# Where tiles lie in SBUF modulo 512 bytes, and where the last projection's tiles live

## The chip, the cores and the metric

The kernel runs on one core of one Trainium2 chip. The metric is the device time of one execution in microseconds, the median of repeated runs. One further execution was taken by the hardware profiler, and all rows below are from it.

## The reference

A decoder trunk of two layers on 256 tokens of width 2048. Each layer is `h <- LayerNorm(alpha * h + W_out(gate * mixer(h)))`. Layer 0 is a gated linear recurrence (HGRN2), layer 1 native sparse attention: compressed, selected and windowed keys, whose three outputs are summed under gates. With 256 tokens there are four blocks of 64, so the selection takes them all.

```
def _hgrn2_mixer(x, w_in, g_norm, w_out, lower_bound):
    q, f_logit, v, z = jnp.split(x @ w_in, 4, axis=-1)          # w_in 2048 x 8192
    log_f = jnp.logaddexp(jnp.log(lower_bound), jnp.log1p(-lower_bound) + jax.nn.log_sigmoid(f_logit))
    k = -jnp.expm1(log_f)
    ...                                                          # the recurrence, head by head
    o = o * lax.rsqrt(jnp.mean(o * o, -1, keepdims=True) + RMS_EPS)
    return (o.reshape(B, S, D) * g_norm * jax.nn.silu(z)) @ w_out    # w_out 2048 x 2048

def _nsa_mixer(x, cos, sin, w_in, cmp_pos_k, cmp_w1_k, cmp_w2_k, cmp_pos_v, cmp_w1_v, cmp_w2_v, w_out):
    q, k_c, v_c, k_s, v_s, k_w, v_w, gate_logit, z = jnp.split(x @ w_in, ...)   # w_in 2048 x 7216
    ...
    o = gate(0) * o_cmp + gate(1) * o_slc + gate(2) * o_win
    return (o * jax.nn.silu(z)) @ w_out                          # w_out 2048 x 2048

for i in range(DEPTH):                                           # DEPTH = 2
    h = _layer_norm(DEEPNORM_ALPHA * h + mixer_i(h), ln_g, ln_b)
```

## The kernel before

**Products.** Every product with a weight matrix is done in three passes. An fp32 operand is split into a part `hi` (rounded to fp32r by ScalarE, line 79) and a part `lo = x - hi` (VectorE, line 80), and the product is hi·hi + hi·lo + lo·hi. The weights come in blocks of 256 rows by 512 columns: `load` (line 103) issues one DMA of 512 KB on SP's queue into a `wr` tile, `parts` (line 137) splits it into `wh` and `wl`. One such block is called a j-block here, and a projection has eight of them.

There are two kinds of projection. `project` (line 150, matmuls in lines 146 to 148, and `project_by_tile` likewise) puts tokens on the output's partitions: the activations are the stationary operand, loaded by a weight load of 128x128, and the weights stream past as the moving operand, 512 columns a matmul and twelve matmuls a j-block. `project_t` (line 189, matmuls in lines 201, 203 and 204) puts features on the partitions: the weights are stationary and the activations stream, 256 columns a matmul and 24 matmuls a j-block. The weight load of a matmul runs while the matmul before it streams. So at any time TensorE reads two tiles, one of weights and one of activations.

**Pools and places.** Pools without `side` stack up from the low end of SBUF in the order in which they are opened; those with `side="right"` stack down from the high end. A tag's slots are as large as the largest tile that ever asks for the tag. The *place* of a tile is its byte address in a partition modulo 512. The allocator gives the kernel before these places:

- `acts` (activations, hi and lo of both layers): all slots at 64, 4096 bytes each.
- `wts`: the three `wr` slots at 160. The five `wh` slots at 160, 192, 224, 256, 288 and the five `wl` slots at 320, 352, 384, 416, 448. They step by 32 because `summed` (line 856) asks for 2 x 516 columns under these tags, 4128 bytes, which is eight times 512 plus 32.
- `wide`, in layer 0 and the first product of layer 1: a fourth `wr` and three more `wh` and `wl` slots, in layer 0 all at 160. `slot` (line 127) goes round over the five and the three, so in layer 0 each of a projection's eight j-blocks has its own pair of slots. The order in which they are visited is, as wh/wl: 160/320, 288/448, 256/416, 192/352, 224/384, then three times 160/160.
- `kv`, layer 1: `keys` at 288 and 32, `vals` at 288. In attention `keys` stream against `qT` (at 64), and `pt` (at 256) streams against `vals`.

The *distance* of a matmul is the place of the tile that it streams minus the place of the tile whose weight load runs meanwhile, modulo 512. For instance a matmul of line 147 that streams a `wl` at 320, while activations at 64 are loaded, has distance 256; one of line 201 that streams activations at 64 while a `wh` at 160 is loaded has distance 416. Weights and activations 256 bytes apart give the distance 256 in either kind of projection.

A `wh` tile of the projections with n = 280 columns (lines 705 to 729) has its second row 1120 bytes after the first.

**The order of the work.** The tile framework orders instructions by a timeline simulation of its own, by program order as priority; splits run 300 places ahead (`AHEAD`). SP's queue is served in order, and an issue that waits for its tile holds up all that stand behind it.

**The last projection.** The output projection of layer 1 (lines 873 to 939) works on four column groups c of 512. For c = 0 to 2 it is `project`, c = 3 is `project_by_tile` with `summed`, which needs the splits of all eight j-blocks to be held for a second pass over them. `fetch(c)` (line 838) loads the residual's columns `xr` and two broadcast rows `gb` on SP's queue and applies the rows on GpSimd (lines 846, 847); `gb` has one buffer, `xr` two, in the pool `n1` that takes the place of the attention's pools. After c = 1 `widen()` opens the pool `wide` again (a fourth `wr`, three more `wh` and `wl`), and `row` loads the layer norm's gain and bias, 1 MB each when broadcast. At that stage the activations `hT` in `acts` (tags `ah`, `al`) have been read for the last time.

## Time and profile before

| | |
|---|---|
| median of 3 runs | 1005.46 us (1005.45 to 1005.57) |
| profiled execution | 1005.65 us, of it span 1003.9 us |
| TensorE: matmul (PE) | busy 988.1 us, 98% |
| TensorE: weight load (PEld) | busy 877.3 us, 87% |
| VectorE (DVE) | busy 675.4 us, 67% |
| ScalarE (ACT) | busy 545.3 us, 54% |
| GpSimd (POOL) | busy 118.1 us, 12% |
| granted TensorE clock, mean | 0.997 |
| DMA | 185.25 MB, mean 185 GB/s |

A matmul's end is modelled in the profile and lies after the start of the next one, so the busy time of one matmul (some 390 ns for 512 columns) is longer than the pitch from start to start (some 230 ns). Differences of pitch appear as differences of the mean duration.

### The profile page before, as it was taken

Reading aid. Unit: us, or ns where it says so; the run is one execution under the profiler, and the core shown is the slowest. Engines: PE = TensorE matmul, PEld = TensorE weight load, DVE = VectorE, ACT = ScalarE, POOL = GpSimd, SP = SyncE. Lnnn points to the kernel's source line nnn. Section 1 sums busy time; section 2 is a strip of 40 time slices with the busy share of each in tenths; the row PEclk is TensorE's granted clock in tenths of the full one; section 3 lists DMA queues with packets and bytes.
Section 4 is the critical chain, followed back from the end, with each engine's and each line's share of the span. In section 5 each row is a group of like instructions: output and inputs, shape, how many; then the busy total and the mean of one; then the engine's idle time right before and its main releaser. Section 6 shows DMA issues by size and latency. Waiting matters only on the chain.

```text
span 1003.9 us, 15938 instructions
## 1 busy us (share of the span) xinstructions
PE 988.1 (98%) x6041; PEld 877.3 (87%) x6041; DVE 675.4 (67%) x1123; ACT 545.3 (54%) x872; POOL 118.1 (12%) x180
## 2 busy tenths in 40 slices
PE   8999999999999999999999999999999999999995
PEld 8988998899889988888889888999989889998775
DVE  6796668666765677656575665565858568775578
ACT  6654455444544554434386655554857667775240
POOL 0400300030003000310011020102020022000440
PEclk9999999999999999999999999999999999999998
DMA  8775456556555555457466776666454455345872
GB/s 299 257 232 165 151 180 177 162 155 187 170 166 159 178 179 155 163 172 265 137 217 231 236 241 218 176 209 171 127 167 140 149 154 149 116 142 186 316 247 84
DMA packets 100780, 185.25 MB, mean 185 GB/s; under 512 B 6096, under 2 KB 20512, under 8 KB 100192
## 3 DMA queue, kind: packets, MB, share of 16 engines
q1 hardware_dynamic: 99232, 178.67, 56.7%
q0 software_dynamic: 1472, 5.56, 1.7%
q8 instruction: 47, 0.77, 0.3%
q14 instruction: 29, 0.24, 0.1%
HBM read 180.02 MB, written 4.19 MB: 183 GB/s over the span
## 4 chain that ended last, share of the span: by engine, by line
PE 90%; DMA 4%; DVE 3%; POOL 1%; issue 1%; ACT 1%; SPq 0%; DVEq 0%; POOLq 0%
PE pjb L146 16%; PE pjb L148 16%; PE pjb L147 16%; PE pjb L201 10%; PE pjb L204 10%; PE pjb L203 10%; PE mxb L441 2%; DMA wr<-in_l_w_out_dram 2%; DMA gb<-in_l_ln_g_dram 1%; PE mxb L214 1%; PE mxb L564 1%; PE mxb L565 1%; PE mxb L566 1%; PE mxb L795 1%; DVE wl L80 1%; PE mxb L614 1%
## 5 line engine op out<-in xcount | busy, mean ns | idle before, releaser
L80 DVE TENSOR_TENSOR wl<-wr,wh 128x1024 fp32r<-128x1024 f32 (+2 forms) x305 | 369.5, 1217 | 186.8 <-ACT wh L79 185.2
L79 ACT ACTIVATE wh<-wr 128x1024 fp32r<-128x1024 f32 (+2 forms) x305 | 316.8, 1043 | 307.4 <-PE pjb L148 163.8
L201 PE MATMUL pjb<-ah,wh 128*128 128x256 f32 x832 | 235.1, 284 | 1.4 <-ACT wh L79 1.4
L204 PE MATMUL pjb<-ah,wl 128*128 128x256 f32 x832 | 233.9, 283 | 0.5 <-DVE wl L80 0.5
L203 PE MATMUL pjb<-al,wh 128*128 128x256 f32 x832 | 234.0, 282 | 0.0
L146 PE MATMUL pjb<-wh,ah 128*128 128x512 f32 (+1 forms) x576 | 221.4, 385 | 0.0
L148 PE MATMUL pjb<-wh,al 128*128 128x512 f32 (+1 forms) x576 | 221.2, 384 | 0.0
L147 PE MATMUL pjb<-wl,ah 128*128 128x512 f32 (+1 forms) x576 | 221.0, 384 | 0.0
L201 PEld LDWEIGHTS pjb<-ah,wh 128*128 128x128 f32 x832 | 156.8, 189 | 2.4 <-ACT wh L79 1.9
L203 PEld LDWEIGHTS pjb<-al,wh 128*128 128x128 f32 x832 | 157.0, 189 | 0.5
L204 PEld LDWEIGHTS pjb<-ah,wl 128*128 128x128 f32 x832 | 156.3, 189 | 1.2 <-DVE wl L80 1.1
L148 PEld LDWEIGHTS pjb<-wh,al 128*128 128x128 f32 x576 | 108.2, 188 | 22.0
L146 PEld LDWEIGHTS pjb<-wh,ah 128*128 128x128 f32 x576 | 108.2, 188 | 21.1
L147 PEld LDWEIGHTS pjb<-wl,ah 128*128 128x128 f32 x576 | 108.3, 188 | 20.9
L147 PE MATMUL pjb<-wl,bh 128*128 128x512 f32 (+2 forms) x272 | 104.5, 385 | 2.2 <-DVE wl L80 1.9
L148 PE MATMUL pjb<-wh,bl 128*128 128x512 f32 (+2 forms) x272 | 103.6, 382 | 0.0
L146 PE MATMUL pjb<-wh,bh 128*128 128x512 f32 (+2 forms) x272 | 102.6, 383 | 0.3 <-ACT wh L79 0.3
L147 PEld LDWEIGHTS pjb<-wl,bh 128*128 128x128 f32 x272 | 51.1, 188 | 14.9 <-DVE wl L80 4.8
L146 PEld LDWEIGHTS pjb<-wh,bh 128*128 128x128 f32 x272 | 51.1, 188 | 11.2 <-ACT wh L79 0.8
L148 PEld LDWEIGHTS pjb<-wh,bl 128*128 128x128 f32 x272 | 51.2, 188 | 10.3
L504 POOL TENSOR_TENSOR gz<-gz,gn 128x512 f32<-128x512 f32 x8 | 13.6, 1702 | 314.6 <-ACT gz L503 314.1
L80 DVE TENSOR_TENSOR wl<-ws,wh 128x1024 fp32r<-128x1024 f32 (+2 forms) x33 | 28.2, 863 | 18.4 <-ACT wh L79 18.2
(229 smaller groups left out, 1055.8 us busy)
## 6 DMA issues: line engine op xcount, KB each, us to landing
wr<-in_l_w_in_dram SPq DMA_DIRECT2D x218, 512.0 KB, 3.8
wr<-in_l_w_out_dram SPq DMA_DIRECT2D x64, 512.0 KB, 4.5
ws<-in_l_w_in_dram SPq DMA_DIRECT2D x12, 512.0 KB, 4.5
wr<-in_l_cmp_w_k_dram SPq DMA_DIRECT2D x5, 512.0 KB, 4.0
wr<-in_l_cmp_w_v_dram SPq DMA_DIRECT2D x5, 512.0 KB, 3.9
wr<-in_l_w_in_dram SPq DMA_DIRECT2D x9, 280.0 KB, 3.3
xr<-in_x_dram POOLq DMA_DIRECT2D x4, 512.0 KB, 5.3
norm<-hb POOLq DMA_DIRECT2D x2, 1024.0 KB, 5.5
```

Source lines behind the costliest of these rows:

```text
L79: act.activation(hi, src, AF.Copy)
L80: dve.tensor_tensor(lo, src, hi.bitcast(F32), op=OP.subtract)
L146: pe.matmul(ps, xh, wh, start=(k == 0), stop=False)
L147: pe.matmul(ps, xh, wl, start=False, stop=False)
L148: pe.matmul(ps, xl, wh, start=False, stop=(k == KT - 1))
L201: pe.matmul(o, hi[:, kk, c], xh, start=(k == 0 and b % 2 == 0), stop=False, skip_group_check=True)
L203: pe.matmul(o, hi[:, kk, c], xl, start=False, stop=False, skip_group_check=True)
L204: pe.matmul(o, lo[:, kk, c], xh, start=False, stop=(k == KT - 1), skip_group_check=True)
L214: last[0] = pe.transpose(ps[:, i], src[:, i], ident).ins
L441: pe.matmul(ps[:, h], km[:, h].rearrange("p b r j -> p (b r j)"), later, start=True, stop=True)
L504: pool.tensor_tensor(z, z, gn, op=OP.mult)
L564: pe.matmul(o, a[0], b[0], start=start, stop=False)
```

## The change

- A pool `edge` of 160 bytes is opened at the right edge ahead of `wts`, and `parts` asks for `wh` and `wl` tiles of always 1024 columns, of which it uses the first n of each row. With `summed` gone from these tags their slots have 4096 bytes, eight times 512. So `wr`, `wh` and `wl`, those of `wide` too, all come to place 320: 256 bytes from the activations at 64. In the projections with 280 columns the second row moves to the same place as the first.
- Two gaps in `kv` (320 and 448 bytes) put `keys` at 192 and 448 and `vals` at 0, which is 256 from `pt`.
- The last group: `summed` takes its tiles from a new pool `late` with eight slots each for `wh` and `wl`, opened in the place where `widen()` stood. Its rows have 576 columns, its second half begins at column 320. `wide` is not opened again: from c = 2 on there are three `wr` slots instead of four, and for c = 2 five `wh` and `wl` instead of eight.
- The output projection's loads: `xr` and `gb` of `fetch` become tiles of `acts` under the tag `al` (four slots, so two fetches fit), the layer norm's gain and bias become two halves each under the tag `ah`, loaded by four DMAs of 512 KB instead of two of 1 MB.

No arithmetic is changed. `room` allocates a tile that nothing writes or reads.

```
--- before.py
+++ after.py
@@ -62,6 +62,13 @@
 
     consts = ctx.enter_context(tc.tile_pool(name="consts", bufs=1))
     acts = ctx.enter_context(tc.tile_pool(name="acts", bufs=4))
+
+
+    def room(p, n):
+
+        p.tile([128, n // 4], F32, name=f"room{n}")
+
+    room(ctx.enter_context(tc.tile_pool(name="edge", bufs=1, side="right")), 160)
     wts = ctx.enter_context(tc.tile_pool(name="wts", bufs=5, side="right"))
     pj = ctx.enter_context(tc.tile_pool(name="pj", bufs=4, space=PSUM))
     mx = ctx.enter_context(tc.tile_pool(name="mx", bufs=4, space=PSUM))
@@ -135,8 +142,8 @@
         return p.tile(shape, dtype, name=name, tag=name, bufs=b)
 
     def parts(raw):
-        hi = slot(list(raw.shape), F32R, "wh", 5, 3)
-        lo = slot(list(raw.shape), F32R, "wl", 5, 3)
+        k, n = raw.shape[1:]
+        hi, lo = (slot([128, k, 1024 // k], F32R, name, 5, 3)[:, :, 0:n] for name in ("wh", "wl"))
         with tc.high_priority(AHEAD):
             split(hi, lo, raw)
         return hi, lo
@@ -663,6 +670,7 @@
         kv_pool = attention.enter_context(tc.tile_pool(name="kv", bufs=1, side="right"))
 
         keys = [kv_pool.tile([128, 4, 528], F32R, name=f"keys{i}") for i in range(2)]
+        room(kv_pool, 320)
         vals = [kv_pool.tile([128, NT, 2, 512], F32R, name=f"vals{i}") for i in range(2)]
 
 
@@ -671,6 +679,7 @@
         for v in pcs:
             act.activation(v, ident[:, 0:1, None, None].to_broadcast([128, 2, 2, 64]), AF.Copy, scale=0.0)
         gates = kv_pool.tile([128, NT, 48], F32, name="gates")
+        room(kv_pool, 448)
         ck = Compression(cp, "k")
         ck.flatten(xk)
         xv = cp.tile([128, 4, S], F32, name="xv", tag="xk")
@@ -835,11 +844,11 @@
     stats = n1.tile([128, NT, 8, 6], F32, name="stats", bufs=1)
 
 
+
     def fetch(c):
         cs = slice(512 * c, 512 * (c + 1))
-        xr = n1.tile([128, NT, 512], F32, name="xr")
+        xr, gb = (acts.tile([128, 2, 512], F32, name=name, tag="al") for name in ("xr", "gb"))
         nc.sync.dma_start(xr, norm0[:, cs].rearrange("(t p) d -> p t d", p=128))
-        gb = n1.tile([128, 2, 512], F32, name="gb", bufs=1)
         for i, name in enumerate(("l0_ln_g", "l0_ln_b")):
             nc.sync.dma_start(gb[:, i], a[name][None, cs].to_broadcast([128, 512]))
         for t in range(NT):
@@ -848,27 +857,27 @@
         return xr
 
     def row(name):
-        r = n1.tile([128, D], F32, name=name, bufs=1)
-        nc.sync.dma_start(r, a[name][None, :].to_broadcast([128, D]))
-        return r
-
+        r = [acts.tile([128, D // 2], F32, name=name, tag="ah") for _ in range(2)]
+        for i, v in enumerate(r):
+            nc.sync.dma_start(v, a[name][None, D // 2 * i:D // 2 * (i + 1)].to_broadcast([128, D // 2]))
+        return lambda b, e: r[b * 2 // D][:, b % (D // 2):b % (D // 2) + e - b]
 
     def summed(raw):
 
 
-        parts = [slot([128, 2, 516], F32R, name, 5, 3) for name in ("wh", "wl")]
+        parts = [late.tile([128, 2, 576], F32R, name=name) for name in ("wh", "wl")]
         ws = n1.tile([128, 2], F32, name="ws")
         with tc.high_priority(AHEAD):
-            split(*(bass.AP(tensor=v.tensor, offset=v.offset, ap=[v.ap[0], [516, 2], [258, 2], [1, 256]])
+            split(*(bass.AP(tensor=v.tensor, offset=v.offset, ap=[v.ap[0], [576, 2], [320, 2], [1, 256]])
                     for v in parts), raw.rearrange("p k (u n) -> p k u n", u=2))
             dve.tensor_reduce(ws, raw[:, :, 256:512], axis=AX.X, op=OP.add)
             split(*(v[:, :, 256:258] for v in parts), ws[:, :, None].to_broadcast([128, 2, 2]))
 
         def halves(v, kk):
-            return bass.AP(tensor=v.tensor, offset=v.offset + 516 * kk, ap=[v.ap[0], [258, 2], [1, 256]])
+            return bass.AP(tensor=v.tensor, offset=v.offset + 576 * kk, ap=[v.ap[0], [320, 2], [1, 256]])
 
         return [[halves(v, kk) for v in parts] + [v[:, kk, 0:258] for v in parts] +
-                [v[:, kk, 258:514] for v in parts] for kk in range(2)]
+                [v[:, kk, 320:576] for v in parts] for kk in range(2)]
 
     for c in range(4):
         cs = slice(512 * c, 512 * (c + 1))
@@ -891,12 +900,12 @@
         def centred(t, m, *parts):
             for a, b in parts:
                 h = hb[:, t, a:b]
-                dve.scalar_tensor_tensor(h, h, m, g1[:, a:b], op0=OP.subtract, op1=OP.mult)
+                dve.scalar_tensor_tensor(h, h, m, g1(a, b), op0=OP.subtract, op1=OP.mult)
 
         def scaled(t, r, *parts):
             for a, b in parts:
                 h = hb[:, t, a:b]
-                dve.scalar_tensor_tensor(h, h, r, b1[:, a:b], op0=OP.mult, op1=OP.add)
+                dve.scalar_tensor_tensor(h, h, r, b1(a, b), op0=OP.mult, op1=OP.add)
                 nc.sync.dma_start(y[128 * t:128 * (t + 1), a:b], h)
 
         def finish(t, ps, other=None):
@@ -931,12 +940,11 @@
             if c == 2:
                 last_xr = fetch(3)
             if c == 1:
-                widen()
+                late = ctx.enter_context(tc.tile_pool(name="late", bufs=8, side="right"))
                 g1, b1 = row("l1_ln_g"), row("l1_ln_b")
         else:
             xr.append(last_xr)
             project_by_tile(oT, a["l1_w_out"], 512 * c, finish, summed=summed)
-    wide.close()
 
 
 # ---- launch: one core; inputs and outputs as the reference has them ----
```

## Rows read from the trace of the kernel before

**Rows 1.** The page: busy time of the engines, and the chain that ended last.

```profile
PE 988.1 (98%) x6041; PEld 877.3 (87%) x6041; DVE 675.4 (67%) x1123; ACT 545.3 (54%) x872; POOL 118.1 (12%) x180
...
PE 90%; DMA 4%; DVE 3%; POOL 1%; issue 1%; ACT 1%; SPq 0%; DVEq 0%; POOLq 0%
```

**Rows 2.** Matmuls by line and shape: count, busy us, mean ns, idle before.

```profile
L201 PE MATMUL pjb<-ah,wh 128*128 128x256 f32 x832 | 235.1, 284 | 1.4 <-ACT wh L79 1.4
...
L146 PE MATMUL pjb<-wh,ah 128*128 128x512 f32 x512 | 202.6, 396 | 0.0
...
L147 PE MATMUL pjb<-wl,bh 128*128 128x512 f32 x240 | 95.6, 398 | 2.2 <-DVE wl L80 1.9
```

**Rows 3.** Timeline of PE, layer 0: first matmul of each j-block of one `project_t`.

```profile
132.50 0.28 PE L201 MATMUL pjb<-ah,wh 128*128 128x256 f32 x1
...
135.33 0.28 PE L201 MATMUL pjb<-ah,wh 128*128 128x256 f32 x1
...
138.16 0.28 PE L201 MATMUL pjb<-ah,wh 128*128 128x256 f32 x1
...
140.99 0.28 PE L201 MATMUL pjb<-ah,wh 128*128 128x256 f32 x1
...
143.82 0.29 PE L201 MATMUL pjb<-ah,wh 128*128 128x256 f32 x1
...
146.71 0.28 PE L201 MATMUL pjb<-ah,wh 128*128 128x256 f32 x1
...
149.59 0.28 PE L201 MATMUL pjb<-ah,wh 128*128 128x256 f32 x1
...
152.47 0.28 PE L201 MATMUL pjb<-ah,wh 128*128 128x256 f32 x1
...
155.35 0.40 PE L146 MATMUL pjb<-wh,ah 128*128 128x512 f32 x1
```

**Rows 4.** Groups in 53.86 to 56.63 us, the j-block with slots 160/320.

```profile
L146 PE MATMUL pjb<-wh,ah 128*128 128x512 f32 x4 | 1.6, 397 | 0.0
L148 PE MATMUL pjb<-wh,al 128*128 128x512 f32 x4 | 1.6, 397 | 0.0
L147 PE MATMUL pjb<-wl,ah 128*128 128x512 f32 x4 | 1.6, 390 | 0.0
```

**Rows 5.** The same in 72.89 to 75.67 us, a j-block with slots 160/160.

```profile
L148 PE MATMUL pjb<-wh,al 128*128 128x512 f32 x5 | 2.0, 394 | 0.0
L146 PE MATMUL pjb<-wh,ah 128*128 128x512 f32 x4 | 1.6, 399 | 0.0
L147 PE MATMUL pjb<-wl,ah 128*128 128x512 f32 x4 | 1.6, 392 | 0.0
```

**Rows 6.** Groups in 917 to 985 us, the last projection.

```profile
L147 PE MATMUL pjb<-wl,bh 128*128 128x512 f32 x87 | 34.9, 401 | 2.2 <-DVE wl L80 1.9
...
L146 PE MATMUL pjb<-wh,bh 128*128 128x258 f32 x9 | 2.5, 282 | 0.0
```

**Rows 7.** Stages of the end: us; PE, PEld, DVE, ACT, POOL busy; clock, DMA share, GB/s.

```profile
893.00:917.00 24.00, 24.00 (x119) 19.76 (x118) 13.38 (x22) 14.45 (x27) 0.00 (x0) 1.00 0.52 170
917.00:940.00 23.00, 22.17 (x95) 17.33 (x93) 10.49 (x18) 8.84 (x10) 5.04 (x4) 1.00 0.84 292
```

**Rows 8.** Waits of SP's queue from 880 us: total us, times, longest.

```profile
SPq L844 <- POOL xr L847: 11.4, 3, 5.4
...
SPq L841 <- DVE bl L80: 4.1, 1, 4.1
```

**Rows 9.** Timeline of SP's queue in the same stretch.

```profile
924.06 0.47 SPq L852 DMA_DIRECT2D l_ln_g<-in_l_ln_g_dram  x1
924.57 1.39 SPq L852 DMA_DIRECT2D l_ln_b<-in_l_ln_b_dram  x1
...
959.43 0.34 SPq L844 DMA_DIRECT2D gb<-in_l_ln_g_dram  x1
```

**Rows 10.** What ScalarE's splits waited for, from 915 us.

```profile
ACT wh L79 <- DMA wr<-in_l_w_out_dram: 33.4, 16, 12.0
```

More of the change, by code (lines that the diff above doesn't have):

```diff
@@ L64, in trunk, with room @@
     acts = ctx.enter_context(tc.tile_pool(name="acts", bufs=4))
+    def room(p, n):
+        p.tile([128, n // 4], F32, name=f"room{n}")
+    room(ctx.enter_context(tc.tile_pool(name="edge", bufs=1, side="right")), 160)
     wts = ctx.enter_context(tc.tile_pool(name="wts", bufs=5, side="right"))
@@ L137, in parts @@
     def parts(raw):
-        hi = slot(list(raw.shape), F32R, "wh", 5, 3)
-        lo = slot(list(raw.shape), F32R, "wl", 5, 3)
+        k, n = raw.shape[1:]
+        hi, lo = (slot([128, k, 1024 // k], F32R, name, 5, 3)[:, :, 0:n] for name in ("wh", "wl"))
         with tc.high_priority(AHEAD):
@@ L665, in trunk @@
         keys = [kv_pool.tile([128, 4, 528], F32R, name=f"keys{i}") for i in range(2)]
+        room(kv_pool, 320)
         vals = [kv_pool.tile([128, NT, 2, 512], F32R, name=f"vals{i}") for i in range(2)]
@@ L673, in trunk @@
         gates = kv_pool.tile([128, NT, 48], F32, name="gates")
+        room(kv_pool, 448)
         ck = Compression(cp, "k")
@@ L839, in fetch @@
         cs = slice(512 * c, 512 * (c + 1))
-        xr = n1.tile([128, NT, 512], F32, name="xr")
+        xr, gb = (acts.tile([128, 2, 512], F32, name=name, tag="al") for name in ("xr", "gb"))
         nc.sync.dma_start(xr, norm0[:, cs].rearrange("(t p) d -> p t d", p=128))
-        gb = n1.tile([128, 2, 512], F32, name="gb", bufs=1)
         for i, name in enumerate(("l0_ln_g", "l0_ln_b")):
@@ L850, in row @@
     def row(name):
-        r = n1.tile([128, D], F32, name=name, bufs=1)
-        nc.sync.dma_start(r, a[name][None, :].to_broadcast([128, D]))
-        return r
+        r = [acts.tile([128, D // 2], F32, name=name, tag="ah") for _ in range(2)]
+        for i, v in enumerate(r):
+            nc.sync.dma_start(v, a[name][None, D // 2 * i:D // 2 * (i + 1)].to_broadcast([128, D // 2]))
+        return lambda b, e: r[b * 2 // D][:, b % (D // 2):b % (D // 2) + e - b]
     def summed(raw):
-        parts = [slot([128, 2, 516], F32R, name, 5, 3) for name in ("wh", "wl")]
+        parts = [late.tile([128, 2, 576], F32R, name=name) for name in ("wh", "wl")]
         ws = n1.tile([128, 2], F32, name="ws")
         with tc.high_priority(AHEAD):
-            split(*(bass.AP(tensor=v.tensor, offset=v.offset, ap=[v.ap[0], [516, 2], [258, 2], [1, 256]])
+            split(*(bass.AP(tensor=v.tensor, offset=v.offset, ap=[v.ap[0], [576, 2], [320, 2], [1, 256]])
                     for v in parts), raw.rearrange("p k (u n) -> p k u n", u=2))
@@ L867, in halves @@
         def halves(v, kk):
-            return bass.AP(tensor=v.tensor, offset=v.offset + 516 * kk, ap=[v.ap[0], [258, 2], [1, 256]])
+            return bass.AP(tensor=v.tensor, offset=v.offset + 576 * kk, ap=[v.ap[0], [320, 2], [1, 256]])
         return [[halves(v, kk) for v in parts] + [v[:, kk, 0:258] for v in parts] +
-                [v[:, kk, 258:514] for v in parts] for kk in range(2)]
+                [v[:, kk, 320:576] for v in parts] for kk in range(2)]
     for c in range(4):
@@ L893, in centred @@
                 h = hb[:, t, a:b]
-                dve.scalar_tensor_tensor(h, h, m, g1[:, a:b], op0=OP.subtract, op1=OP.mult)
+                dve.scalar_tensor_tensor(h, h, m, g1(a, b), op0=OP.subtract, op1=OP.mult)
         def scaled(t, r, *parts):
@@ L898, in scaled @@
                 h = hb[:, t, a:b]
-                dve.scalar_tensor_tensor(h, h, r, b1[:, a:b], op0=OP.mult, op1=OP.add)
+                dve.scalar_tensor_tensor(h, h, r, b1(a, b), op0=OP.mult, op1=OP.add)
                 nc.sync.dma_start(y[128 * t:128 * (t + 1), a:b], h)
@@ L933, in trunk @@
             if c == 1:
-                widen()
+                late = ctx.enter_context(tc.tile_pool(name="late", bufs=8, side="right"))
                 g1, b1 = row("l1_ln_g"), row("l1_ln_b")
@@ L938, in trunk @@
             project_by_tile(oT, a["l1_w_out"], 512 * c, finish, summed=summed)
-    wide.close()
 _INS = ["x", "xT", "positions", "hgrn_lb_logits", "l0_w_in", "l0_g_norm", "l0_w_out", "l0_ln_g", "l0_ln_b",
```

## The prediction

> **What bounds the kernel now.** I read the page first: TensorE is busy 98% of the span, no other engine over 67%, and of the chain that ended last 90% is TensorE, 4% DMA [rows 1]. So only two things can move the time by much: the pitch of the matmuls, and the places where TensorE waits.
>
> The groups of matmuls come next [rows 2]. Two shapes make up nearly all: the 128x512 ones of lines 146 to 148, 3 x (512 + 240) = 2256 of them, and the 128x256 ones of lines 201, 203 and 204, 3 x 832 = 2496. The reader should see that lines 146 and 201 wait for nothing worth naming (1.4 us in 832), so that their mean durations are a matter of streaming, not of waiting.
>
> Then the timeline of one projection of layer 0 in which nothing is interleaved [rows 3]. Eight j-blocks of 24 identical matmuls take 2.83, 2.83, 2.83, 2.83, 2.89, 2.88, 2.88 and 2.88 us. At the granted clock of 1.00 [rows 7], that is 2.4 GHz, 24 x 256 columns would stream in 2.56 us, so every block is 10 to 13% above that. The blocks differ in nothing but the slots in which their weights lie: by the order of the slots the first is 160/320, the last three are 160/160. Between these two only the place of `wl` differs. A third of the matmuls, those of line 203, which stream `al` while `wl` is loaded, are at distance 256 in the first and at 416 in the last, and the block is 0.05 us shorter. Slot places do change the pitch; the question is what the distance 256 for all of them gives, which no block before has.
>
> The same is seen in the other kind of projection. In a block with slots 160/320 the matmuls of line 147, at distance 256, last 390 ns, and their neighbours of lines 146 and 148, at 96, 397 ns [rows 4]. In a block with 160/160 all three are at 96 and last 399, 392 and 394 ns [rows 5]. A block's 256-column pitch is 2.856 / 24 = 119 ns on average and its mean duration 283 or 284 ns [rows 2, 3], so the modelled end adds some 164 ns, and a 512-column duration of 396 ns is a pitch of 232 ns.
>
> Last, the end. From 917 to 985 us three lines of 86 or 87 matmuls with 512 columns and some 26 with 258 run [rows 6]; at 232 and 119 ns they need 63.5 of the 68 us, so 4.5 us are lost there. ScalarE's splits wait 33.4 us for loads of `w_out` there, 12.0 us at the longest [rows 10], while the DMA engines go from 52% to 84% busy [rows 7]. SP's queue explains it: the 1 MB rows of the layer norm go out at 924 us, ahead of loads that are due, and line 844's `gb`, with one buffer, blocks the queue three times, 11.4 us in all, until GpSimd has finished with the fetch before [rows 8, 9].
>
> **The change part by part.**
>
> *128x256 matmuls, distance 256 for all.* There are 832 / 8 = 104 blocks. Eight projections in layer 0 average (155.35 - 132.50) / 8 = 2.856 us [rows 3]; the five of layer 1 use the first five slots alone, (4 x 2.83 + 2.89) / 5 = 2.842; together 2.851. One bound takes the 0.05 us of the third that is at 256 three times: 2.88 - 0.15 = 2.73, a gain of 0.12 x 104 = 12.5 us. The other bound: the three blocks with one distance for all of their matmuls (416) are among the slowest, so one distance for all may lock into a slow rhythm, 2.88, a loss of 3.0 us. Four mixed blocks stand at 2.83. I take 2.81, about half of the extrapolation: **-4.3 us**.
>
> *128x512 matmuls, distance 256.* Against the mean of 396 to 398 ns [rows 2] the 390 ns of rows 4 would be 6.5 ns x 2256 = 14.7 us; that is one bound. But line 147 has 392 ns at distance 96 too [rows 5], so part of its lead is the line's, not the distance's. The bound on the other side is line 146's 399 ns [rows 5], +2.5 ns, +5.6 us. I take half of the 7 ns between neighbours in rows 4, 3.5 ns x 2256: **-7.9 us**. All of this passes to the end one for one while TensorE is the chain; should the last projection stay bound by its loads, the 0.9 us of its 260 matmuls are lost.
>
> The 280- and 258-column matmuls, the compression's, and those of `keys` and `vals` are a tenth of the others in number; at 3 ns either way they are under 1.5 us together, taken as nothing. The `room` tiles issue nothing. The splits keep their sizes; VectorE and ScalarE, at 67 and 54% [rows 1], cover what places may do to them: even 2% of VectorE's 675 us would be hidden by its idle time.
>
> Here one rule speaks against the whole step. Rows 3 show identical matmuls taking 2.83 or 2.88 us by their slots alone. The Trainium skill ("SBUF — State Buffer", section "Who interferes with whom") holds that TensorE has two independent read ports, one for the moving operand and one for weight loads, and that it never waits on anyone. The rows disagree with that; by the rule the two steps above would be zero instead of -12.2 us.
>
> *The last group's slots.* `late` gives c = 3 sixteen tiles that nobody else uses, so its splits no longer wait for c = 2's matmuls to release theirs. Given up are the fourth `wr` and, for c = 2, three of eight pairs. Five pairs hold 5 x 12 x 0.232 = 14 us of matmuls, against the longest wait of 12.0 us [rows 10]: still covered, by little.
>
> *The loads.* `xr` and `gb` for c = 0 and 1 and the rows need only slots of `hT`, free when `project_t` of gate 3 has ended, ahead of 893 us, while before line 841 waited 4.1 us for the last split of `o` [rows 8] and all went out at 922 to 925. Four more megabytes then move through a stretch with 52% DMA [rows 7] instead of one that is full. `gb` no longer waits for GpSimd, so the `wr` loads behind it in SP's queue, and ScalarE's and VectorE's splits behind those, go out up to 11.4 us earlier in sum. The rows cost two more issues of some 0.5 us each on SP's queue [rows 9], hidden while `wr` runs three loads ahead. The cost if the cover is gone: the same burst with the shorter `wr` ring loses what is lost now. Of the 4.5 us lost I expect 3 back (bounds: all 4.5 back; 4.5 more lost): **-3.0 us**. After 985 us VectorE sets the end with the layer norm's last pass, and nothing changes there.
>
> Sum: -4.3 - 7.9 - 3.0 = -15.2. The profiled execution took 1005.65 us (span 1003.9), 0.2 above the median of the runs: 1005.5 - 15.2 = **990.3 us**.
>
> **Rivals.**
>
> *Places don't matter, only the end does.* The differences in rows 3 could come from the mix of places, or from what ScalarE and VectorE write meanwhile, and return as others. Against it: the three blocks 160/160 take 2.88 us each. Then -3.0 alone: 1002.5 us; without the end's gain 1005.5, no change. The skill's rule above leads to the same times.
>
> *Slower: one distance for all locks into a slow rhythm.* For it: the three blocks of one distance are 0.05 us slower than the mixed ones. Price: +3.0 and +5.6 as worked out, less the end's 3.0: 1011 us. It decides as soon as the 24-matmul block is over 2.85 us and the 12-matmul block over 12 x 0.232 = 2.79 us.
>
> *The whole extrapolation holds.* -12.5 - 14.7 - 4.5: 974 us. Against it: the nearest mixed blocks show a third of it.
>
> *The end gets worse* (shorter rings in the burst): +4.5 instead of -3.0, 998 us, within the first case's range.
>
> **How the numbers follow.** My forecast, 979 to 1001 us, the last rival in it: 0.60. The whole extrapolation, below 979: 0.07. Only the end, 1001 to 1003.4: 0.10. Nothing at all: 0.10. Slower: 0.13. A measurement of this kernel tells some 0.2%, 2 us, from no change; so faster 0.77, same 0.10, slower 0.13. The range leaves out the slow case and most of the extreme one: 978 to 1006 us.
>
> **What would show it.** Right: in a projection without interleaving all eight j-blocks take the same, near 2.81 us with `project_t` and 2.75 with `project`; lines 146 to 148 lie at 392 to 393 ns, lines 201 to 204 at 281 to 282; line 844 waits for GpSimd no more, the layer norm's rows go out before 915 us, and the matmuls from 917 to 985 lose under 2 us. Wrong: blocks at 2.88 again (locking), or unequal blocks although all places agree (the distance is not the cause), or new waits of line 147 for `wl` in c = 1 and 2 (the shorter rings).

## The result and the profile after

The median fell from 1005.46 to 999.08 us (six runs each, 997.59 to 1001.92 after, 1005.01 to 1005.57 before). The ratio is 0.9938, with a 95% interval of 0.9928 to 0.9949. The forecast was 990.3, in a range of 978 to 1006: the direction was right, the size less than half of what was forecast. The profiled execution took 999.29 us with a span of 997.6.

The busy times of the changed kernel, from the page, to be held against [rows 1]:

```profile
PE 981.8 (98%) x6041; PEld 882.6 (88%) x6041; DVE 683.2 (68%) x1123; ACT 545.4 (55%) x872; POOL 116.2 (12%) x180
```

TensorE still sets the time. The groups of matmuls by line and shape, which answer to [rows 2] (lines 201, 203, 204 are now 208, 210, 211; lines 146 to 148 are 153 to 155):

```profile
L208 PE MATMUL pjb<-ah,wh 128*128 128x256 f32 x832 | 236.8, 285 | 0.5 <-ACT wh L86 0.5
L210 PE MATMUL pjb<-al,wh 128*128 128x256 f32 x832 | 236.2, 285 | 0.0
L211 PE MATMUL pjb<-ah,wl 128*128 128x256 f32 x832 | 235.3, 285 | 0.5 <-DVE wl L87 0.5
...
L153 PE MATMUL pjb<-wh,ah 128*128 128x512 f32 x512 | 200.2, 392 | 0.0
L153 PE MATMUL pjb<-wh,bh 128*128 128x512 f32 x240 | 94.6, 394 | 1.0 <-ACT wh L86 1.0
```

The 512-column matmuls went from 396 to 392 ns, as forecast (392 to 393). The 256-column ones went from 284 to 285, where 281 to 282 was forecast. They became slower. The timeline of the same `project_t` as in [rows 3], first matmuls of the first two j-blocks and of the last, then the first two j-blocks of the `project` behind it (all eight blocks of `project_t` start 2.88 apart):

```profile
131.84 0.28 PE L208 MATMUL pjb<-ah,wh 128*128 128x256 f32 x1
...
134.72 0.28 PE L208 MATMUL pjb<-ah,wh 128*128 128x256 f32 x1
...
152.00 0.28 PE L208 MATMUL pjb<-ah,wh 128*128 128x256 f32 x1
...
154.88 0.40 PE L153 MATMUL pjb<-wh,ah 128*128 128x512 f32 x1
...
157.63 0.39 PE L153 MATMUL pjb<-wh,ah 128*128 128x512 f32 x1
...
160.35 0.39 PE L153 MATMUL pjb<-wh,ah 128*128 128x512 f32 x1
```

The equal blocks show that places do set the pitch: eight different blocks became eight alike. But they are all 2.88 us, the slowest that before had. A `project` block takes 2.75 and then 2.72 us; before, the same two took 2.79 and 2.78. In a block of 2.72 us of an earlier `project` (56.76 to 59.48 us) the three lines have one duration, where [rows 4, 5] show 390 to 399:

```profile
L155 PE MATMUL pjb<-wh,al 128*128 128x512 f32 x5 | 1.9, 389 | 0.0
L153 PE MATMUL pjb<-wh,ah 128*128 128x512 f32 x4 | 1.6, 389 | 0.0
L154 PE MATMUL pjb<-wl,ah 128*128 128x512 f32 x4 | 1.6, 389 | 0.0
```

The last projection starts 6 us sooner and then waits in another place. Its stages, in the columns of [rows 7]:

```profile
893.00:905.00 12.00, 9.89 (x50) 7.78 (x49) 9.20 (x13) 6.70 (x10) 5.27 (x4) 1.00 0.89 329
905.00:923.00 18.00, 16.25 (x65) 12.71 (x64) 10.56 (x12) 8.29 (x12) 2.92 (x2) 0.91 0.52 171
923.00:940.00 17.00, 17.00 (x76) 14.08 (x75) 11.34 (x15) 7.12 (x7) 3.99 (x3) 1.00 0.71 219
940.00:980.00 40.00, 39.66 (x189) 33.18 (x188) 30.41 (x55) 15.20 (x22) 2.96 (x3) 1.00 0.48 157
```

TensorE is idle 3.9 us between 893 and 923 us. The granted clock is 0.91 in 905 to 923, a mean of stretches at 2.4 and at 1.2 GHz: behind the last of those waits, from 918.5 to 921.5 us, seven matmuls of 512 columns start 427 ns apart instead of 227. From 923 us on almost nothing is lost, where the kernel before lost 4.5 us from 917 to 985. The rows lead to ScalarE's and SP's queues. SP's queue now sends the layer norm's rows and two fetches ahead of 890 us (924 in [rows 9]); four of its issues:

```profile
865.17 0.46 SPq L862 DMA_DIRECT2D l_ln_g<-in_l_ln_g_dram  x1
...
889.18 0.89 SPq L862 DMA_DIRECT2D l_ln_b<-in_l_ln_b_dram  x1
...
907.95 0.37 SPq L851 DMA_DIRECT2D xr<-norm  x1
908.42 15.59 SPq L113 DMA_DIRECT2D wr<-in_l_w_out_dram  x5
```

In ScalarE's queue splits of `w_out` stand ahead of attention's last steps and wait for the loads behind that burst; what stands behind such a split starts only when it is nearly done, and TensorE waits 1.1 us for one of these steps, line 816's `o`. The brackets give the idle time before an instruction and what ended it:

```profile
894.82 1.06 ACT L86 ACTIVATE wh<-wr 128x1024 fp32r<-128x1024 f32 x1 [3.96 <-DMA wr<-in_l_w_out_dram]
895.79 0.58 ACT L816 ACTIVATE o<-mxb 128x512 f32<-128x512 f32 x1
...
914.80 1.06 ACT L86 ACTIVATE wh<-wr 128x1024 fp32r<-128x1024 f32 x1 [5.65 <-DMA wr<-in_l_w_out_dram]
```

From 880 us the waits of SP's queue and of ScalarE, answering to [rows 8, 10]:

```profile
SPq L851 <- POOL xr L856: 7.1, 2, 4.2
...
ACT wh L86 <- DMA wr<-in_l_w_out_dram: 33.9, 18, 5.7
```

The wait of `gb` for GpSimd (11.4 us) is gone, but `xr`, which now shares four slots with `gb`, waits 7.1 us for GpSimd instead. ScalarE's longest wait for a load fell from 12.0 to 5.7 us; their sum from 880 us on did not fall (33.7 us before).

The account, by the starts of all matmuls in the two traces (one execution each), where a pitch is counted up to 260 ns (512 columns) or 150 ns (256) and what is above as waiting (matmuls at the lower clock add to it):

| us | before | after | measured | forecast |
|---|---|---|---|---|
| 512-column matmuls | 525.5 | 515.3 | -10.2 | -7.9 |
| 256-column matmuls | 297.7 | 300.9 | +3.2 | -4.3 |
| TensorE waiting in the last projection | 4.5 | 6.7 | +2.3 | -3.0 |
| from TensorE's last matmul to the span's end | 10.6 | 9.7 | -0.8 | 0 |
| start of the first projection's matmuls, and all else | | | -0.8 | 0 |
| span | 1003.9 | 997.6 | -6.3 | -15.2 |

### The profile page after: what moved, and what is told of

It is laid out like the page before. It is cut to its first block, busy times and chain, and to the rows that moved or that the text cites. A ratio compares the mean times of both kernels' runs of the same rounds, so it can differ in the third digit from the quotient of the medians.

```text
span 997.6 us, 15935 instructions
## 1 busy us (share of the span) xinstructions
PE 981.8 (98%) x6041; PEld 882.6 (88%) x6041; DVE 683.2 (68%) x1123; ACT 545.4 (55%) x872; POOL 116.2 (12%) x180
## 4 chain that ended last, share of the span: by engine, by line
PE 87%; DVE 5%; DMA 4%; ACT 2%; issue 1%; SPq 1%; POOL 0%; DVEq 0%; ACTq 0%; POOLq 0%
PE pjb L154 16%; PE pjb L155 16%; PE pjb L153 16%; PE pjb L208 9%; PE pjb L211 9%; PE pjb L210 9%; DMA wr<-in_l_w_out_dram 3%; DVE wl L87 3%; PE mxb L448 2%; PE mxb L221 1%; ACT wh L86 1%; PE mxb L571 1%; PE mxb L572 1%; PE mxb L573 1%; PE mxb L804 1%
## 5 line engine op out<-in xcount | busy, mean ns | idle before, releaser
L153 PE MATMUL pjb<-wh,ah 128*128 128x512 f32 (+1 forms) x576 | 219.0, 381 | 0.0
L155 PE MATMUL pjb<-wh,al 128*128 128x512 f32 (+1 forms) x576 | 218.9, 380 | 0.0
L208 PEld LDWEIGHTS pjb<-ah,wh 128*128 128x128 f32 x832 | 159.4, 192 | 1.3 <-ACT wh L86 0.9
L211 PEld LDWEIGHTS pjb<-ah,wl 128*128 128x128 f32 x832 | 158.9, 192 | 1.0 <-DVE wl L87 0.9
L210 PEld LDWEIGHTS pjb<-al,wh 128*128 128x128 f32 x832 | 159.3, 192 | 0.4
```

What stands on the lines that cost most here:

```text
L153: pe.matmul(ps, xh, wh, start=(k == 0), stop=False)
L155: pe.matmul(ps, xl, wh, start=False, stop=(k == KT - 1))
L208: pe.matmul(o, hi[:, kk, c], xh, start=(k == 0 and b % 2 == 0), stop=False, skip_group_check=True)
L210: pe.matmul(o, hi[:, kk, c], xl, start=False, stop=False, skip_group_check=True)
L211: pe.matmul(o, lo[:, kk, c], xh, start=False, stop=(k == KT - 1), skip_group_check=True)
```

## The experiments

Two theories stood at the start. By the first, the distance of the two tiles that TensorE reads sets the pitch, and 256 is good for `project` and bad for `project_t`. By its rival, one distance for all matmuls locks `project_t` into 2.88 us whatever it is, as the three blocks 160/160 had suggested; a second rival came up on the way, that the place of a single tile counts, not the distance. For the end, the question was which part of the move loses the time.

### The end alone

The places are those of before again, the `late` slots and the moved loads stay. One block of the first `project_t` asks for 516 columns, so that the slots keep the 4128 bytes that `summed` gave them.

```
-    room(ctx.enter_context(tc.tile_pool(name="edge", bufs=1, side="right")), 160)
...
-        hi, lo = (slot([128, k, 1024 // k], F32R, name, 5, 3)[:, :, 0:n] for name in ("wh", "wl"))
+        hi, lo = (slot(list(raw.shape), F32R, name, 5, 3) for name in ("wh", "wl"))
...
-            hi, lo = slot([128, 2, 512], F32R, "wh", 5, 3), slot([128, 2, 512], F32R, "wl", 5, 3)
+            hi, lo = (slot([128, 2, 512 if j else 516], F32R, v, 5, 3)[:, :, 0:512] for v in ("wh", "wl"))
...
-        room(kv_pool, 320)
...
-        room(kv_pool, 448)
```

> All slots of the weights, the keys and the values lie where they lay before the change (wh 160 to 288, wl 320 to 448, wide at 160); the pool late and the moved loads stay. Theory A (the gain is the pitch at distance 256 alone, and the moved loads cost something): blocks as in the kernel before (24 matmuls of project_t 2.83 to 2.88 us), the waits of TensorE between 890 and 925 us as in the changed kernel, so 1005 to 1008 us, no gain or a loss. Theory B (the last group's slots and the moved loads give the gain): 999 to 1002 us.

Measured: 1005.95 us (1003.47 to 1008.84, ten runs) beside 1005.27, ratio 0.9999 (0.9989 to 1.001). The 512- and 256-column sums are those of before, 525.6 and 297.8 us. So the gain comes from the places, and the end gives nothing by itself. In the profiled run, the slowest of the ten (1008.84 us), 8.1 us are lost in the last projection, most of it between 900 and 928 us.

### The moved loads held back, and spread

First, each fetch is issued behind the fourth load of its group, and the four halves of the rows within group 2. Here `issued[0]` is the latest load of `w_out` so far, and `due` issues one half of the gain or the bias. Then, in a second kernel, fetches and halves are issued one by one over groups 0 to 2: `DUE` names the group and the j-block behind whose load one goes out, 4 stands for a half and 0 to 3 for a fetch.

```
             if j == 3:
-                xr.append(fetch(c))
+                with tc.issue_after(issued[0]):
+                    xr.append(fetch(c))
+            if c == 2 and j % 2:
+                due()
...
```

```
+    DUE = {(0, 0): 4, (0, 2): 0, (0, 5): 4, (0, 7): 1, (1, 1): 4, (1, 4): 4, (1, 6): 2, (2, 4): 3}
...
```

> The changed kernel, but on SP's queue each fetch stands behind the fourth weight load of its own column group (the one of the last group behind group 2's eighth), and the layer norm's gain and bias go out in four parts behind the second, fourth, sixth and eighth load of group 2. Theory A (the burst of 4 MB of fetches and rows between 864 and 895 us holds up the weight loads, and through ScalarE's queue the attention's own steps): the waits of TensorE between 890 and 925 us, some 6 us, go, no stretch of TensorE at a lower granted clock is left there, 993 to 996 us. Theory B (those waits come from the shorter rings of three wr and five wh and wl): they stay, 998 to 1002 us.

> The changed kernel with its places (weights at 320), but the 6 MB beside the weights spread over SP's queue: each part stands behind one named weight load of the last projection (halves of the layer norm's rows behind loads 0 and 5 of group 0 and 1 and 4 of group 1; the fetches behind load 2 and 7 of group 0, 6 of group 1, 4 of group 2), some 8 us apart, none closer than 0.5 to 1 MB. Pinned into group 2 the same loads only moved the waits to 956 to 970 us. Theory A (the waits come from several of these loads going out together, wherever they stand): the waits of TensorE after 885 us fall from 6.7 to under 3 us, 994 to 996 us. Theory B (three wr and five wh and wl don't cover the stretch, with or without a burst): 6 us or more stay lost, 998 to 1001 us.

Measured: held back 1000.74 us (ratio 0.9955, 0.994 to 0.997), spread 999.25 (0.9935, 0.992 to 0.995). The changed kernel is at 0.9938 (0.9928 to 0.9949): neither differs from it by more than the intervals. The waits did not vanish, they moved. The stages of the two, in the columns of [rows 7], first held back:

```profile
893.00:923.00 30.00, 29.89 (x140) 24.36 (x140) 19.70 (x21) 15.27 (x19) 6.38 (x4) 1.00 0.57 181
...
956.00:973.00 17.00, 13.03 (x49) 9.17 (x47) 12.16 (x22) 6.93 (x12) 4.37 (x4) 0.90 0.72 234
```

Then spread:

```profile
893.00:923.00 30.00, 30.00 (x141) 24.79 (x141) 19.24 (x25) 15.95 (x21) 6.03 (x4) 1.00 0.75 246
...
956.00:973.00 17.00, 14.35 (x59) 10.28 (x57) 14.94 (x28) 7.77 (x14) 0.00 (x0) 1.00 0.56 186
```

TensorE's idle time of 893 to 923 us is gone in both, and 2.7 to 4.0 us stand in 956 to 973 instead, at the start of the last group.

### Other places for the weights

One number is changed; activations stay at 64. `room` of 0, 96, 64, 128 and 32 bytes puts the weights at 480, 384, 416, 352 and 448. The pools stacked below the weights, `kv` among them, move along with them; the sums below count the projections alone.

```
-    room(ctx.enter_context(tc.tile_pool(name="edge", bufs=1, side="right")), 160)
+    room(ctx.enter_context(tc.tile_pool(name="edge", bufs=1, side="right")), 96)
```

> The changed kernel without the 160 bytes at the right edge: all weights at place 480, so distance 416 in project and 96 in project_t, one distance for all matmuls of a kind. Theory A (one distance for all locks project_t at its columns and 32 cycles whatever the distance): blocks of 24 in project_t at 2.88 us as in the changed kernel; blocks of 12 in project at 2.72. Theory B (the distance sets the pitch, and 96 is a bad one, as it was for project): project_t 2.95 us or more, project near 2.75; the whole 1006 us or more.

> The changed kernel with 96 instead of 160 bytes at the right edge: all weights at place 384, so distance 320 in project and 192 in project_t. Theory A (one distance for all locks project_t whatever the distance): blocks of 24 at 2.88 us, of 12 at 2.72. Theory B (the distance sets the pitch; 192 was among the fastest for project_t in the mixed blocks of the kernel before): blocks of 24 at 2.80 to 2.82 us, blocks of 12 at 2.73 to 2.77; the whole 995 to 999 us.

> The changed kernel with 64 bytes at the right edge: weights at place 416, distance 352 in project and 160 in project_t. Theory A (each kind's pitch is set by its own distance): project_t as at 192, 2.82 to 2.83 us per 24 (160 and 192 were the fastest in the mixed blocks), project slower than at 320, 2.76 to 2.80 us per 12; in all 993 to 998 us. Theory B (project_t has two states and only 192 is in the fast one): 2.88 us per 24, and over 1000 us.

> The changed kernel with 128 bytes at the right edge: weights at place 352, distance 288 in project and 224 in project_t, between the changed kernel's (256, 256: 2.72 and 2.88 us) and place 384's (320, 192: 2.75 and 2.83 us). Theory A (pitch changes smoothly with distance): 2.73 and 2.85 us, in all 995 to 998. Theory B (steps): project at 2.72 or 2.75, project_t at 2.88 or 2.83, in all between 990 and 1001; the best case, 2.72 and 2.83, would beat both by some 5 us.

> Weights at 448, activations at 64: distances 384 and 128, weights on a multiple of 64. By the distance alone project should lie between its neighbours at 352 (2.800) and 416 (2.811), 2.80 to 2.81, and project_t between 96 (2.880) and 160 (2.815), about 2.85; time about 1007. By the alignment of the moving weights project should be 2.72 to 2.75 and the time 992 to 998.

Measured, one execution each: 1011.18, 992.74, 1004.87, 1004.75 and 1004.94 us. The fastest, with weights at 384, has 2.83 us from start to start in a `project_t` and 2.75 in the `project` behind it:

```profile
150.03 0.28 PE L208 MATMUL pjb<-ah,wh 128*128 128x256 f32 x1
...
152.86 0.40 PE L153 MATMUL pjb<-wh,ah 128*128 128x512 f32 x1
...
171.84 0.39 PE L153 MATMUL pjb<-wh,ah 128*128 128x512 f32 x1
...
174.59 0.39 PE L153 MATMUL pjb<-wh,ah 128*128 128x512 f32 x1
```

What each place does to undisturbed j-blocks stands in the table below. The theory that one distance for all locks `project_t` at 2.88 fell here: it takes 2.815 at one uniform distance and 2.84 at another. The expectations came in part. At 480 `project` takes 2.81 us, slower than either theory had it, and `project_t` 2.88, not the 2.95 of the second. At 416 the blocks came, but the whole takes 7 us more than the 993 to 998 expected. At 352 `project` takes 2.80 us, more than at its neighbours 320 (2.72) and 384 (2.75), so the pitch does not change smoothly from one distance to the next.

### Both operands moved: distance or place?

So far the fast places of the weights, 320 and 384, were multiples of 64 and most of the slow ones were not. Here activations move to 96 as well.

```
+    shifted = ctx.enter_context(tc.tile_pool(name="shifted", bufs=1))
     acts = ctx.enter_context(tc.tile_pool(name="acts", bufs=4))
...
-    room(ctx.enter_context(tc.tile_pool(name="edge", bufs=1, side="right")), 160)
+    room(ctx.enter_context(tc.tile_pool(name="edge", bufs=1, side="right")), 128)
+    room(shifted, 32)
```

(with 96 in place of 128 in the second one)

> Every tile of the left pools, activations first, lies 32 bytes higher (96 instead of 64 modulo 512), and the weights at 352 instead of 320: the distance stays 256, as in the changed kernel, but neither operand stands on a multiple of 64 bytes any more. If the distance alone sets the pitch, project's j-block stays at 2.720 us and project_t's 24-block at 2.880, the 512-column matmuls sum to about 515 us, the 256-column ones to 301, and the time is that of the changed kernel, 997 to 1002. If the fast places (320, 384) were fast because the moving weights stood on a multiple of 64 and the slow ones (160, 352, 416, 480) because they did not, project goes to 2.80, the 512-column matmuls to 527 us, and the time to about 1010.

> Activations at 96 and weights at 384: the distance is 288 in project and 224 in project_t, that of the run with weights at 352, but the weights stand on a multiple of 64. If the distance alone sets the pitch: project 2.80, project_t 2.84, time 1004.8 as in that run. If the alignment of the moving weights does: project 2.72 to 2.75, the 512-column matmuls 515 to 520 us, time 993 to 998.

Measured: 999.52 and 1005.31 us, as the distance has it. The timelines of PE: the last j-block of a `project_t`, then the first and second of the `project` behind it. Distance 256, as in the changed kernel, with weights at 352:

```profile
151.73 0.28 PE L210 MATMUL pjb<-ah,wh 128*128 128x256 f32 x1
...
154.61 0.40 PE L155 MATMUL pjb<-wh,ah 128*128 128x512 f32 x1
...
157.36 0.39 PE L155 MATMUL pjb<-wh,ah 128*128 128x512 f32 x1
...
160.08 0.39 PE L155 MATMUL pjb<-wh,ah 128*128 128x512 f32 x1
```

Distance 288, with weights at 384:

```profile
152.28 0.28 PE L210 MATMUL pjb<-ah,wh 128*128 128x256 f32 x1
...
155.12 0.39 PE L155 MATMUL pjb<-wh,ah 128*128 128x512 f32 x1
...
157.91 0.39 PE L155 MATMUL pjb<-wh,ah 128*128 128x512 f32 x1
...
160.71 0.39 PE L155 MATMUL pjb<-wh,ah 128*128 128x512 f32 x1
```

Distance 288 again, with weights at 352 and activations at 64:

```profile
151.90 0.28 PE L208 MATMUL pjb<-ah,wh 128*128 128x256 f32 x1
...
154.74 0.39 PE L153 MATMUL pjb<-wh,ah 128*128 128x512 f32 x1
...
157.54 0.39 PE L153 MATMUL pjb<-wh,ah 128*128 128x512 f32 x1
...
160.34 0.39 PE L153 MATMUL pjb<-wh,ah 128*128 128x512 f32 x1
```

The first gives 2.88, 2.75, 2.72 us, to a hundredth the changed kernel; the second and third give 2.84, 2.79 or 2.80, and 2.80. The same weights' place, 352, is fast at one distance and slow at another. At the two distances tried in this way the distance sets the pitch, not the place.

The table puts together the undisturbed j-blocks of all these runs, in us, the sums over the run, in the manner of the account above, and the time of the profiled execution:

| distance in `project` | its block | distance in `project_t` | its block | 512-column sum | 256-column sum | time |
|---|---|---|---|---|---|---|
| 256 (two kernels) | 2.72 | 256 | 2.88 | 515 | 301 | 999.3; 999.5 |
| 288 (two kernels) | 2.80 | 224 | 2.84 | 527 | 297 | 1004.8; 1005.3 |
| 320 | 2.75, at first 2.80 | 192 | 2.83, a few 2.72 | 519 | 292 | 992.7; 995.9 |
| 352 | 2.80 | 160 | 2.815 | 528 | 296 | 1004.9 |
| 384 | 2.78 to 2.80 | 128 | 2.85 | 526 | 298 | 1004.9 |
| 416 | 2.81 | 96 | 2.88 | 529 | 301 | 1011.2 |
| before: mixed | 2.77 to 2.80 | mixed | 2.82 to 2.88 | 525.5 | 297.7 | 1005.65 |

### Weights at 384, timed, and with spread loads

The first is the kernel above with `room` of 96; the second adds the spread loads to it.

> The kernel that was fastest in one look (992.74), weights at 384, now timed. Its 512-column matmuls summed to 519.3 us and its 256-column ones to 292.4 (515.3 and 300.9 in the changed kernel), its waits at the end to 4.9. If the look was typical, the median is 991.5 to 995, the ratio to the kernel before 0.986 to 0.990. If the waits at the end vary as they do in the changed kernel (4.3 to 7.6), up to 996.

> Weights at place 384 together with the spread loads. If places and loads are two causes that add, it is faster than place 384 alone (992.7 us) by as much as the spread gains at place 320: 988 to 990 us if that is 4 us, 992 to 993 if it is nothing. Blocks as at place 384, 2.83 and 2.75 us.

Measured: 994.33 us (991.75 to 995.93), ratio 0.9872 (0.9849 to 0.9895); with the loads spread 995.91, ratio 0.9906 (0.989 to 0.9923), no better. The profiled runs of one and the same kernel, 992.74 and 995.93, have the same sums (519 and 292) and lost 4.9 and 8.0 us in the last projection, so these two differ by the end alone. The same stage of both, first the faster, after much the same waits between 881 and 905 us:

```profile
905.00:923.00 18.00, 16.45 (x71) 12.90 (x70) 9.55 (x13) 8.82 (x10) 0.00 (x0) 1.00 0.64 202
...
905.00:923.00 18.00, 15.57 (x60) 12.11 (x59) 9.05 (x12) 7.76 (x9) 0.00 (x0) 0.91 0.52 170
```

By the starts of its matmuls the faster one waits 0.9 and 1.0 us from 910 us on and stays at 2.4 GHz. The slower one waits 1.8 and 1.0 us there, and behind that its matmuls start 427 ns apart for some 3 us, at 1.2 GHz.

### The loads not moved

`xr`, `gb` and the rows stay in `n1`, so SP's queue has the order of before. For that only four `late` slots of each kind have room; the control has four as well, with the loads moved.

```
-                late = ctx.enter_context(tc.tile_pool(name="late", bufs=8, side="right"))
+                late = ctx.enter_context(tc.tile_pool(name="late", bufs=4, side="right"))
```

```
-        xr, gb = (acts.tile([128, 2, 512], F32, name=name, tag="al") for name in ("xr", "gb"))
+        xr = n1.tile([128, NT, 512], F32, name="xr")
+        gb = n1.tile([128, 2, 512], F32, name="gb", bufs=1)
...
-        r = [acts.tile([128, D // 2], F32, name=name, tag="ah") for _ in range(2)]
+        r = n1.tile([128, D], F32, name=name, bufs=1)
...
```

> The changed kernel with four late slots each for wh and wl instead of eight; loads moved as there. A control for the next run, which has no room for eight. If the depth of the late slots matters, the last group has to wait for its own matmuls to release slots, and the time rises by 1 to 4 us over the changed kernel, to 1000 to 1003. If it does not, 997.5 to 1001.5, as the changed kernel.

> As the run before (places at 320, four late slots), but xr, gb, the gain and the bias stay in the pool n1, with one gb buffer and the two 1 MB rows of the kernel before, so SP's queue has the order of before. In the changed kernel TensorE lost 6.7 us in the last projection, in the kernel before 4.5. If the moved loads' burst at 864 to 895 us is what loses the time there, this run loses about 4.5 and takes 995 to 998, 1.5 to 3 us less than the control. If the time is lost because TensorE comes to the last projection 6 us sooner while the same bytes have to arrive, this run loses 6 to 10 us as well and takes 998 to 1003.

> The same with the weights at 384. If the burst is the cause, about 4.5 us lost at the end and 989 to 992, ahead of the 994.3 of place 384 with moved loads. If the earlier arrival is the cause, 992 to 997.

Measured: the control 1004.56 us (ratio 0.9991, 0.9981 to 1.0001), the loads not moved 1008.20 (1.0028, 1.0018 to 1.0037), the same with weights at 384 1003.71 (0.9983, 0.9974 to 0.9992). All three lie above their expected times. The theory that the burst costs the time fell: without the moved loads it is 3.6 us longer than the control. TensorE loses 6.8 us there as well, later, with the DMA engines 87% busy; two stages of the run, in the columns of [rows 7]:

```profile
893.00:920.00 27.00, 27.00 (x129) 22.30 (x128) 16.74 (x22) 14.78 (x19) 0.00 (x0) 1.00 0.45 145
920.00:943.00 23.00, 21.44 (x93) 16.80 (x92) 10.86 (x20) 5.80 (x6) 11.29 (x8) 1.00 0.87 318
```

The depth of the slots was a surprise. With four, TensorE's last matmul starts at 987.1 us, as with eight (987.9), but the span ends 17.5 us behind it instead of 9.7. Groups of VectorE from 985 us in the control show why:

```profile
L908 DVE SCALAR_TENSOR_TENSOR hb<-hb,mv,l_ln_b 128x512 f32<-128x512 f32 x8 | 5.6, 736 | 0.4 <-POOL mv L249 0.4
L903 DVE SCALAR_TENSOR_TENSOR hb<-hb,mv,l_ln_g 128x512 f32<-128x512 f32 x4 | 3.0, 745 | 0.0
```

In the changed kernel line 908 has five such instructions there, and line 903 none with `mv`: the first token tile's layer norm is done while TensorE works on the second. With four slots it comes behind TensorE's end. Less the 7.8 us that this costs, an estimate from the two ends, the kernels with the loads not moved would take 1000.4 and 995.9 us, in the ranges expected if the earlier arrival is the cause.

### A fourth load slot

The changed kernel gave up the fourth `wr`. Rows of 516 columns in `late`, as before the change, make room for it (the control has them too). Weights at 384.

```
...
+        if name == "wr" and fourth[0]:
+            spare[1] = i = (spare[1] + 1) % 4
+            p, b = (fourth[0], 1) if i == 3 else (wts, n)
+            return p.tile(shape, dtype, name=name, tag=name, bufs=b)
...
-        parts = [late.tile([128, 2, 576], F32R, name=name) for name in ("wh", "wl")]
+        parts = [late.tile([128, 2, 516], F32R, name=name) for name in ("wh", "wl")]
...
+                fourth[0] = late
```

> Weights at 384, loads moved, eight late slots, but their rows have 516 columns as before instead of 576, which makes room for a fourth wr slot (next run). The late slots step by 32 bytes again, so the last group's matmuls run at a mixture of distances; 96 matmuls of 512 columns at up to 6 ns are 0.6 us. Expected: the 994.3 of place 384 within its own spread, 991.5 to 996.

> The run before with a fourth wr slot from c = 2 on, which the changed kernel gave up together with the pool wide. If the weights are late in the last projection because only three loads can be under way, ScalarE's waits for wr there fall from 30 us and TensorE's loss from 5 to 8 us to about 4: 990.5 to 993, 1 to 3 us under the control. If the loss sits ahead of c = 2, where the first loads have to come beside the moved ones, or if the bytes themselves are the limit, no difference.

Measured: control 993.66 us (993.04 to 993.75; ratio 0.9879, 0.9862 to 0.9897), with the fourth `wr` 994.17 (0.9887, 0.987 to 0.9905). No difference; ScalarE waited 40.7 us for loads from 880 us on in the profiled run with it, and 34.7 without. The fourth slot is not what is missing. The control has the lowest median of the timed kernels, but it does not differ from the plain kernel with weights at 384 (0.9872) by more than the intervals.

## Why the prediction was right in direction and too large

**128x512 matmuls: right.** Forecast -7.9 us, measured -10.2. That distance 256 is faster for this kind was read rightly from [rows 4]. The size was a choice, half of what line 147 led by, and there is luck in its coming near: the whole would have been 14.7.

**128x256 matmuls: the step that failed, in its sign.** Forecast -4.3, measured +3.2. I took a third of the matmuls at distance 256 in a mixed block as evidence for 256, and half of the extrapolation, 2.81 us a block. The other bound, 2.88, is what came, and its price of +3.0 us was right. A block of 160/320 was faster for another reason than its matmuls of line 203 at 256: the runs show that 256 and 416 both give 2.88 when uniform, and that the low values lie at 160 to 224. A mixture is no mean of its distances: in the first block of [rows 3] the matmuls of lines 201, 203 and 204 take 116.8, 116.4 and 121.1 ns from start to start, the first and the last at 416 and the second at 256, and in the uniform blocks, at 416 before and at 256 after, all three lines take 120.0. What makes the mixture faster is not shown. The rival "one distance for all locks into a slow rhythm" was half right: it came for one kind of projection and not for the other, and not because all distances are equal, since 160, 192 and 224 are uniform too and take 2.82 to 2.84.

**The end: the second term that failed.** Forecast -3.0; TensorE waited 2.3 us more, and what lies behind its end gave 0.8 back. From the start of the last projection to the span's end it is 111.4 us in both traces (892.5 to 1003.9, 886.2 to 997.6), so what the places had won ahead of it was kept and nothing added. The step's details came: `gb`'s wait vanished, the rows went out before 915 us, the stretch from 917 us on loses under 2 us. But I counted the time lost only where it had been lost before. The loads that go out earlier meet the splits that ScalarE is made to wait for ahead of attention's last steps, at 894.8 and 914.8 us, and TensorE loses 3.9 us there, and behind these waits some 3 us run at 1.2 GHz. Whether held back, spread, or left where they were, 4 to 8 us are lost somewhere.

The size of +2.3 rests on one execution of each kernel, and the two of the kernel with weights at 384 differ by 3.1 us in the same term, so only this is sure: the -3.0 did not come. The other traces bear on why. Counted as in the account, the five slow uniform kernels (weights at 352, 416, 448 and 480, and at 384 with activations at 96) have the same moved loads, reach the last projection at 893 to 899 us and lose 3 to 4 us in it, where the kernel before lost 4.5; all kernels that reach it at 881 to 887 us lose 4 to 8. That fits the theory that TensorE comes sooner while the same bytes have to arrive. But the kernel with the end alone reaches it at 893 us and lost 8.1 in the run that was profiled, its slowest, so this is argued and the cause stays open. By its control, moving the loads is worth 3.6 us, near my 3.0; what the end alone gave back to come out at nothing is not shown. That the fourth `wr` is missing is excluded, at weights of 384 at least.

**Places of `keys` and `vals`, and the bulk of the rest:** taken as nothing, and all that is not in the named terms is -0.8 us, 0.7 of it the first projection's matmuls starting at 4.8 instead of 5.5 us.

**The time.** That 999 us lies within the range is no support for the sum. The 256-column term was off by 7.5 us and the end by 4.5, both to the same side, and the range was wide enough for that. The rival "the end gets worse" (998 us) is near by other terms: it has the 256-column matmuls gain 4.3 us.

Of the other rivals "places don't matter" is refuted by the equal blocks and by the runs at distances 256 and 288. The Trainium skill's rule weighed in the prediction ("SBUF — State Buffer", section "Who interferes with whom", that TensorE's two read ports are independent and it never waits) would have all blocks of a kind in the table take one time. The runs disagree: the blocks of `project` go from 2.72 to 2.81 us, those of `project_t` from 2.815 to 2.88, and the times span 18 us, from 992.7 to 1011.2.

## What to carry to other kernels

When two tiles are read at once by TensorE, their addresses modulo 512 are a knob worth a per cent, and it is one number: sweep it, for every kind of matmul that shares the tiles, instead of arguing from a mixed layout. Here, of the six pairs tried, 320 for `project` and 192 for `project_t` was best (994 us), though 256 was the best for `project` alone. At the end of a kernel that waits for loads, time won by moving loads out of a crowded stretch can come back as a wait elsewhere, as it did here; measure such a move by itself.

## What the runs showed of the hardware

- The pitch of matmuls that wait for nothing depends on the distance modulo 512 bytes between the streamed tile and the tile being loaded, not on the place of either: at distances 256 and 288 both operands moved by 32 bytes gave the same blocks to 0.01 us. That the remainder by 512 counts is seen within a block: the slices that its matmuls read lie multiples of 512 bytes apart (128 columns of four bytes), and in the changed kernel all 24 matmuls of a `project_t` block take 120.0 ns. A remainder by 256 would not do: 160 gives 2.815 us and 416, in the last three blocks of [rows 3], 2.88.
- This holds for layouts in which all matmuls of a kind have one distance. In a mixed block a matmul at 416 took 116.8 or 121.1 ns by its line (lines 201 and 204, first block of [rows 3]), against 120.0 where all are at 416.
- At distance 256 both kinds take 13.3 ns more than their columns at 2.4 GHz: 2.72 us / 12 = 226.7 against 213.3 ns, 2.88 us / 24 = 120.0 against 106.7 ns.
- One distance can have two rhythms. With weights at 384, `project` starts with two blocks of 2.80 us and goes on at 2.75 after a disturbed block, and `project_t` has a few of 2.72 among 2.83: in layer 0 at 120.96, 221.40 and 321.85 us, one repetition of some 100.4 us apart, and at the same blocks in the second profiled execution.
- The Trainium skill ("TensorE: Matmul & The Clock Gate", section "Wait — 56ns, not 53.3ns?") gives 215.7 ns from start to start for 512 columns. No block here reaches it: the shortest mean pitch of a block, with these fp32r operands and a weight load under each matmul, is 226.7 ns.
